# The first stage of a two-layer hybrid step: its own buffer for each scale and shift piece, and the first query and key products taken feature pair by feature pair

## The chip, the cores and the metric

The kernel runs on one core of a Trainium2 chip. The metric is the device time of one execution in microseconds (us); the time before is the median of three executions. The engines have the profile's names: PE multiplies matrices, with its weight loads shown apart as PEld; DVE, ACT and POOL work element by element; SP only issues loads and stores. Each of these runs its own instructions in a fixed order and waits for others through semaphores.

## The reference, cut to what matters

The step computes two layers over 512 latent tokens and 128 context tokens, 640 in all, of 1024 features. Layer 0 is attention, layer 1 a gated linear recurrence, and each is followed by a gated feed-forward block. What the change touches is the beginning of layer 0:

```
m  = silu(cond) @ w_mod + b_mod            # one row of conditions for latent, one for context tokens
shift, scale = first two parts of m        # 1024 each
xm = rms_norm(x, g) * (1 + scale) + shift
q, k, v = split(xm @ w_qkv)
```

`x` has 640 rows of 1024 features. `rms_norm` divides each token by the root of its mean square. Then queries, keys and values are made, 16 heads of 64, and attention follows.

## The kernel before, in words

Features lie on the 128 partitions, so that `x` is 8 tiles (k = 0 to 7) of 128 features by 640 tokens. A product of full precision is made of three products of numbers that are split into a high and a low part: high by high, high by low and low by high. This holds for all projections: the weights (`raw`) are split into `whi` and `wlo`, the tokens into `hi` and `lo` (all four token-wide arrays carry the tag `big` in the profile). A tile of 128 output features takes 8 k x 3 = 24 products for each half of the tokens (320 columns, the constant `CH`), 48 in all; `unit` loads and splits its weights, `some` (lines 214 to 223) makes the products. There are three slots each for `raw`, `whi` and `wlo`.

The first stage is `start` (lines 296 to 370). Its work:

- The features come in eight loads. ACT squares each, DVE adds the squares up (`ssq`). `stat` turns the sum into the root: PE sums over the partitions (`moment`, line 396), DVE scales, POOL takes the power, DVE spreads the result on a diagonal (`dg`), and PE multiplies it by ones so that every partition holds every token's factor (`spread`, line 413). The root is made in two pieces, latent and context, and copied to `ssq` by ACT.
- The scale and shift columns come from 16 pieces of `w_mod` of 512 KB each (`wm0`): four feature pairs (`NB` is 2) by shift or scale (j) by half of the sum (h). A piece is multiplied with the conditions in four small products (line 342), shift and scale in a bank each. The two halves go to `row` through DVE and ACT (lines 353 and 354), four products with `sel` turn the rows into columns (line 357), and small DVE operations give A and B, one column per feature and token kind. The 16 pieces share ten buffers.
- `scaled` gives each feature tile its scale and shift, one step behind the coefficients. Even tiles go through `modulate` on DVE and ACT (lines 418 to 420). Odd tiles are first multiplied by the root on POOL (line 350), then scaled on ACT (line 325) and split (`split`, lines 1076 and 1077).

Then the attention phase opens. `qk(0)` makes the first query tile Q and key tile K, `vq(0)` the first values (lines 236 to 238), and from there `attend(p)` (scores, softmax, output) goes on with `qk(p + 1)` and, at every other step, `vq` made beside it. Queries sit in one buffer with the tag `r`, keys in one with the tag `K` in the attention pool.

Which instruction stands where on each engine is set by the framework's scheduler: it takes program order as priority and orders by a simulated time. In `start` of the kernel before nothing is fixed by hand; `issue_after` is used elsewhere for single instructions.

## Time and profile before

| | |
|---|---|
| median of three executions | 1537.41 us (1535.1 to 1538.31) |
| span of the profiled execution | 1532.6 us |
| PE, DVE, ACT, POOL busy | 1483.2, 1062.8, 695.8, 256.1 us |
| first product of a scale or shift piece; first value product | at 12.8 us; at 57.6 us |

The page gives the span of the profiled execution, from its first to its last instruction; its time outside the span is not listed, and the median is 4.8 us above the span. PE is busy in 97% of the span, and a busy PE is not always PE at its peak, since the granted clock can be lower. In rows in order of time the first number is the start, the second the duration, and the bracket tells how long the engine idled before it and for what. Times of small products include their way through the array, so that the distance between two starts tells more than the duration. A product of plain float32 numbers (lines 342, 357, 396 and 413) shows as two records.

### The profile page before, as it was taken

The page shows a single profiled execution, that of the slowest core. Times are in us where ns is not written, and L with a number is a line of the kernel's source. Part 1 is how long each engine was busy: PE and PEld are TensorE (multiplying, and loading weights), DVE is VectorE, ACT ScalarE, POOL GpSimd, SP SyncE. Part 2 cuts the span into 40 slices and gives each one's busy share as a digit, 9 for nine tenths or more (in the row PEclk, how much of TensorE's full clock was granted, in tenths as well). Part 3 has the DMA queues.
Part 4 walks back from the last instruction along what each step waited for, and adds up shares of the span by engine and source line. Part 5 has one row for each costly group of instructions (what it writes and reads, how often), then busy time and mean ns, then how long its engine had stood idle before and what let it go on. Part 6 is the DMA issues. An engine that isn't in the chain of part 4 may idle for free.

```text
span 1532.6 us, 25990 instructions
## 1 busy us (share of the span) xinstructions
PE 1483.2 (97%) x10309; PEld 1438.5 (94%) x10309; DVE 1062.8 (69%) x2000; ACT 695.8 (45%) x1266; POOL 256.1 (17%) x270
## 2 busy tenths in 40 slices
PE   5999999989999999999999999999899999999997
PEld 4899999879999999999999988799899999999996
DVE  5668888969899888434443869885965656566556
ACT  5566767755333113312331478863534342424242
POOL 2101122100111110000000113230412323222210
PEclk8999999999999999999999999999999999999999
DMA  9545656445566664222223443334332231323221
GB/s 375 155 115 166 185 158 179 147 141 184 177 194 191 192 201 140 73 83 71 76 61 99 153 127 107 107 104 162 113 119 70 83 110 56 99 67 97 70 56 69
DMA packets 73098, 196.65 MB, mean 128 GB/s; under 512 B 8048, under 2 KB 25616, under 8 KB 72848
## 3 DMA queue, kind: packets, MB, share of 16 engines
q1 hardware_dynamic: 58832, 144.48, 30.0%
q0 software_dynamic: 13856, 50.35, 10.8%
q8 instruction: 81, 1.33, 0.4%
q14 instruction: 41, 0.34, 0.1%
q10 hardware_dynamic: 288, 0.16, 0.0%
HBM read 179.48 MB, written 8.92 MB: 123 GB/s over the span
## 4 chain that ended last, share of the span: by engine, by line
PE 85%; DVE 7%; ACT 4%; DMA 2%; issue 2%; SPq 0%; POOL 0%; POOLq 0%; DVEq 0%; ACTq 0%
PE mm L222 14%; PE mm L223 14%; PE mm L221 14%; PE mx L221 5%; PE mx L223 5%; PE mx L222 5%; PE mx L850 3%; PE mx L849 3%; PE mx L851 3%; PE op L687 2%; PE gp L1035 2%; PE tp L611 2%; PE mc L849 1%; PE mc L850 1%; PE mc L851 1%
## 5 line engine op out<-in xcount | busy, mean ns | idle before, releaser
L222 PE MATMUL mm<-big,whi 128*128 128x320 f32 (+3 forms) x1270 | 397.9, 314 | 3.0 <-DVE big L1077 2.1
L221 PE MATMUL mm<-big,whi 128*128 128x320 f32 (+3 forms) x1270 | 394.5, 313 | 3.7 <-ACT big L1076 2.3
L223 PE MATMUL mm<-big,wlo 128*128 128x320 f32 (+3 forms) x1270 | 396.8, 313 | 1.0 <-DVE wlo L182 1.0
L222 PEld LDWEIGHTS mm<-big,whi 128*128 128x128 f32 x1270 | 241.9, 190 | 6.6 <-DVE big L1077 4.4
L221 PEld LDWEIGHTS mm<-big,whi 128*128 128x128 f32 x1270 | 240.3, 190 | 7.5 <-ACT big L1076 2.8
L223 PEld LDWEIGHTS mm<-big,wlo 128*128 128x128 f32 x1270 | 241.5, 190 | 2.5 <-DVE wlo L182 1.4
L250 DVE SCALAR_TENSOR_TENSOR mprod<-mraw,csb 128x1024 f32<-128x1024 f32 x160 | 195.4, 1221 | 11.2 <-DMA mraw<-in_wm 10.7
L443 DVE SCALAR_TENSOR_TENSOR x<-mm,G,x 128x128 f32<-128x128 f32 (+3 forms) x205 | 83.5, 436 | 86.6 <-PE mm L223 86.6
L182 DVE TENSOR_TENSOR wlo<-raw,whi 128x1024 fp32r<-128x1024 f32 (+1 forms) x90 | 110.1, 1224 | 37.4 <-ACT whi L180 22.1
L180 ACT CAST whi<-raw 128x1024 fp32r<-128x1024 f32 (+1 forms) x74 | 76.8, 1037 | 110.1 <-PE mm L222 71.7
L221 PE MATMUL mm<-big,whx 128*128 128x320 f32 (+3 forms) x363 | 113.7, 313 | 0.0
L223 PE MATMUL mm<-big,wlx 128*128 128x320 f32 (+3 forms) x363 | 113.3, 312 | 0.0
L222 PE MATMUL mm<-big,whx 128*128 128x320 f32 (+3 forms) x363 | 113.1, 312 | 0.0
L246 POOL DMA_DIRECT2D mraw<-in_wm x80 | 43.3, 542 | 381.1 <-DVE mprod L250 264.9
L221 PE MATMUL mx<-big,whi 128*128 128x320 f32 (+3 forms) x298 | 93.5, 314 | 0.4 <-ACT big L1076 0.4
L223 PE MATMUL mx<-big,wlo 128*128 128x320 f32 (+3 forms) x298 | 93.0, 312 | 0.0
L222 PE MATMUL mx<-big,whi 128*128 128x320 f32 (+3 forms) x298 | 92.9, 312 | 0.0
L180 ACT CAST whx<-raw 128x1024 fp32r<-128x1024 f32 (+1 forms) x40 | 41.0, 1027 | 93.4 <-PE mm L222 54.2
L221 PE MATMUL mx<-big,whx 128*128 128x320 f32 (+3 forms) x245 | 75.6, 309 | 0.0
L223 PE MATMUL mx<-big,wlx 128*128 128x320 f32 (+3 forms) x245 | 75.5, 308 | 0.0
L1076 ACT CAST whi<-raw 128x1024 fp32r<-128x1024 f32 (+1 forms) x41 | 41.3, 1008 | 74.8 <-PE mm L222 45.0
L222 PE MATMUL mx<-big,whx 128*128 128x320 f32 (+3 forms) x245 | 75.2, 307 | 0.0
(301 smaller groups left out, 3620.8 us busy)
## 6 DMA issues: line engine op xcount, KB each, us to landing
raw<-in_gu SPq DMA_DIRECT2D x88, 512.0 KB, 3.6
mraw<-in_wm POOLq DMA_DIRECT2D x80, 512.0 KB, 4.0
raw<-in_dn SPq DMA_DIRECT2D x24, 512.0 KB, 3.7
raw<-in_wqk SPq DMA_DIRECT2D x16, 512.0 KB, 4.4
raw<-in_wi SPq DMA_DIRECT2D x16, 512.0 KB, 3.6
whi<-in_wi POOLq DMA_DIRECT2D x16, 512.0 KB, 4.0
raw<-in_dn SPq DMA_DIRECT2D x16, 448.0 KB, 3.4
sw<-in_wm SPq DMA_DIRECT2D x10, 512.0 KB, 10.5
```

What stands on the lines that cost most here:

```text
L180: nc.scalar.copy(hi, raw)
L182: nc.vector.tensor_tensor(lo, raw, hi.bitcast(F32), ALU.subtract)
L221: nc.tensor.matmul(ps, hi[:, k], xhi[:, k, s], start=(k == 0), stop=False)
L222: nc.tensor.matmul(ps, hi[:, k], xlo[:, k, s], start=False, stop=False)
L223: nc.tensor.matmul(ps, lo[:, k], xhi[:, k, s], start=False, stop=(k == last))
L246: nc.gpsimd.dma_start(w, self.i["wm"][l * 6 + j - 2, f])
L250: nc.vector.scalar_tensor_tensor(prod, w, 1.0, self.csb[:, s], ALU.mult, ALU.mult, accum_out=out[:, s, f:f + 1])
L443: self.nc.vector.scalar_tensor_tensor(xs, ps[:, a - t0:b - t0], G[:, s, f:f + 1], xs, ALU.mult, ALU.add)
L849: nc.tensor.matmul(ps, hi[:, k], xh[:, k], start=start and k == 0, stop=False, skip_group_check=not start)
L850: nc.tensor.matmul(ps, hi[:, k], xl[:, k], start=False, stop=False, skip_group_check=not start)
L851: nc.tensor.matmul(ps, lo[:, k], xh[:, k], start=False, stop=(k == KH - 1), skip_group_check=not start)
L1076: self.nc.scalar.copy(hi, v)
```

## The change

`start` is rewritten, with these parts:

- Each of the 16 pieces has its own buffer, and all loads are issued ahead: features, the four pieces of the first pair, the weights of the first query tile, first key tile and second query tile, and the other twelve pieces.
- Shift and scale of a pair go into the two halves of one bank, and the coefficients of a pair are made by three operations for both features. The root is made for all five token blocks at once, and the first pair is scaled from the bank that holds it.
- The order on PE, DVE and ACT is written out by hand: `pe`, `dve` and `act` make each instruction follow the one before it in that list on its engine.
- The first two query tiles and the first key tile are multiplied in six banks at once (three tiles by two halves of the tokens), pair by pair: for each pair first all high by high, then high by low, then low by high in two parts. After each of these four parts come the products of one piece of the next pair. Then the next pair's coefficients are made, it is scaled on DVE, cast on ACT, and its products follow.
- `qk` is cut into `queries`, `keys_tile` and the rest, so that `qk(0)` finds Q and K made, and `qk(1)` its query. The tag `r` gets two buffers, K moves to the main pool, and the memory for dynamic load descriptors is set to 4096.

The core of the diff:

```diff
@@ start
+        for k0 in range(0, KT, NB):
+            for j in range(2):
+                for h in range(2):
+                    w = self.t([P, 4, n], F32, f"sw{k0}{j}{h}", 1, sp)
+                    nc.sync.dma_start(w, self.i["wm0"][j, k0 // NB, h])
+                    pieces[k0, j, h] = w
+            if k0 == 0:
+                for f in (0, KT, 1):
+                    raw, whi_, wlo_ = [self.t([P, KT, P], dt, v, 3) for dt, v in ((F32, "raw"), (F32R, "whi"), (F32R, "wlo"))]
+                    nc.sync.dma_start(raw, self.i["wqk"][f])
+                    us.append((whi_, wlo_, raw))
...
+        def pe(step):
+            last["PE"] = order(step, (last.get("PE"),))
...
+        def vectors(k0, pm, j, h):
+            w = pieces[k0, j, h]
+            for k4 in range(4):
+                pe(lambda: nc.tensor.matmul(pm[32 * k4:32 * k4 + 32, j * n:j * n + n], csp[:, 4 * h + k4], w[:, k4], start=(h == 0), stop=(h == 1)))
+
+        def coefficients(k0, pm):
+            row = idle[:, k0 * n:k0 * n + 2 * n]
+            dve(lambda: nc.vector.tensor_copy(row[:, 0:n], pm[:, 0:n]))
+            act(lambda: nc.scalar.copy(row[:, n:2 * n], pm[:, n:2 * n]))
+            pt = self.ps("at")
+            for q in range(2 * NB):
+                pe(lambda: nc.tensor.matmul(pt[:, 2 * q:2 * q + 2], row[:, q * P:q * P + P], sel, start=True, stop=True))
...
+            dve(lambda: nc.vector.tensor_tensor(B, v[:, 0], per(self.col("bsh")), ALU.add))
+            dve(lambda: nc.vector.tensor_tensor(A, v[:, 1], per(b1), ALU.add))
+            dve(lambda: nc.vector.tensor_tensor(A, A, per(self.col("ng00")), ALU.mult))
+            return A, B
...
+        def normed(k, r):
+            dve(lambda: nc.vector.tensor_tensor(self.x[:, k], self.x[:, k], r, ALU.mult))
+
         def scaled(k, A, B):
             for s, a, b in _pieces(0, NTOK):
                 v = self.x[:, k, a:b]
+                dve(lambda: nc.vector.tensor_scalar(v, v, A[:, k % NB, s:s + 1], B[:, k % NB, s:s + 1], ALU.mult, ALU.add))
+            act(lambda: nc.scalar.copy(hi[:, k, 0:NTOK], self.x[:, k, 0:NTOK]))
+
+        def low(k):
+            dve(lambda: nc.vector.tensor_tensor(lo[:, k, 0:NTOK], self.x[:, k, 0:NTOK], hi[:, k, 0:NTOK].bitcast(F32), ALU.subtract))
+
+        def products(k, kind, js=range(6)):
+            for j in js:
+                w, m = us[j // 2][kind == "lh"], (lo if kind == "hl" else hi)
+                s = slice(*CH[j % 2])
+                first, end = kind == "hh" and k == 0, kind == "lh" and k == KT - 1
+                pe(lambda: nc.tensor.matmul(pss[j], w[:, k], m[:, k, s], start=first, stop=end))
+
+        pm = self.ps("ss")
+        vectors(0, pm, 0, 0)
+        bl, dg = root()
+        for j, h in ((0, 1), (1, 0), (1, 1)):
+            vectors(0, pm, j, h)
+        rr = spread(bl, dg)
+        A, B = coefficients(0, pm)
+        whi(0)
+        for k in range(NB):
+            for s, a, b in _pieces(0, NTOK):
+                v = self.x[:, k, a:b]
+                dve(lambda: nc.vector.scalar_tensor_tensor(v, v, A[:, k, s:s + 1], rr[s][:, 0:b - a], ALU.mult, ALU.mult))
+                act(lambda: nc.scalar.activation(hi[:, k, a:b], v, AF.Identity, bias=B[:, k, s:s + 1]))
+        whi(1)
+        r = copied(rr)
+        whi(2)
...
+        for j in range(3):
+            wlo(j)
+        pss = [(self.ps("kk") if j % 2 else self.pg(False))[:, 0:HT] for j in range(6)]
+        for k0 in range(0, KT, NB):
+            more = k0 + NB < KT
+            pm = self.ps("ss") if more else None
+            for step in range(4):
+                if step == 0:
+                    for k in range(k0, k0 + NB):
+                        products(k, "hh")
+                elif step == 1:
+                    for k in range(k0, k0 + NB):
+                        products(k, "hl")
                 else:
+                    for k in range(k0, k0 + NB):
+                        products(k, "lh", range(4) if step == 2 else range(4, 6))
+                if more:
+                    vectors(k0 + NB, pm, step // 2, step % 2)
+            if more:
+                for k in range(k0 + NB, k0 + 2 * NB):
+                    normed(k, r)
+                A, B = coefficients(k0 + NB, pm)
+                for k in range(k0 + NB, k0 + 2 * NB):
+                    scaled(k, A, B)
+                for k in range(k0 + NB, k0 + 2 * NB):
+                    low(k)
+        made = [self.queries(), self.keys_tile(), self.queries()]
+        for j in range(6):
+            t0, t1 = CH[j % 2]
+            made[j // 2][1](t0, slice(t0, t1), pss[j])
+        return [m[0] for m in made]
@@ run
-        with self.phase("start", at=2, rr=1, sc=1, sh=1) as sp:
+        with self.phase("start", at=1, ss=1, kk=3) as sp:
...
-            self.start(xhi, xlo, sp, wbig)
+            Q, K, Q1 = self.start(xhi, xlo, sp, wbig)
...
-            QK = self.qk(0, xhi, xlo, ap)
+            QK = self.qk(0, xhi, xlo, ap, Q, K)
...
-                    QK = self.qk(p + 1, xhi, xlo, ap)
+                    QK = self.qk(p + 1, xhi, xlo, ap, None if p else Q1)
@@ kernel
-    nc = _bacc.Bacc("TRN2", target_bir_lowering=False, num_devices=1)
+    nc = _bacc.Bacc("TRN2", target_bir_lowering=False, num_devices=1, dynamic_dma_scratch_size=4096)
```

`root`, `spread`, `copied`, `whi` and `wlo` do what `moment`, `spread`, line 347 and `unit` did, in the written order.

128 lines of the change are left out of this document (69 added, 59 removed).

## The prediction

> **What bounds the kernel now.** I read the page's first parts, then the stretches of ten microseconds, then the groups and the order of time of the first 60 us. In the page PE is busy nearly throughout:
>
> ```profile
> span 1532.6 us, 25990 instructions
> PE 1483.2 (97%) x10309; PEld 1438.5 (94%) x10309; DVE 1062.8 (69%) x2000; ACT 695.8 (45%) x1266; POOL 256.1 (17%) x270
> ```
>
> The span is 1532.6 us. The median of the three runs, 1537.4 us, is 4.8 us more; I take these 4.8 us as what lies around the span, and they stay. The stretches (length, then busy time of PE, PEld, DVE, ACT and POOL with their instructions, granted clock, DMA share, GB/s) show where PE becomes the bound:
>
> ```profile
> 30.00:40.00 10.00, 8.97 (x49) 6.82 (x48) 6.90 (x12) 6.19 (x9) 0.91 (x1) 0.66 1.02 410
> 40.00:50.00 10.00, 8.19 (x72) 6.12 (x70) 6.94 (x18) 5.83 (x11) 3.65 (x7) 1.00 0.38 117
> 50.00:60.00 10.00, 9.71 (x59) 9.72 (x60) 4.80 (x8) 4.89 (x10) 2.58 (x4) 0.83 0.65 197
> 60.00:70.00 10.00, 10.00 (x87) 10.00 (x86) 7.85 (x28) 5.18 (x9) 0.00 (x0) 1.00 0.57 156
> ```
>
> From 60 us on a stretch has 10.00 of 10.00 us of PE. So what the first stage is worth is the moment by which PE has put a given amount of projection work behind it; later work follows at PE's pace. In the groups of the first 60 us (busy us, then mean ns) the products of the first query and key tiles are counted:
>
> ```profile
> L222 PE MATMUL mm<-big,whi 128*128 128x320 f32 x32 | 12.0, 379 | 0.6 <-DVE big L420 0.6
> L223 PE MATMUL mm<-big,wlo 128*128 128x320 f32 x32 | 11.5, 370 | 1.0 <-DVE wlo L182 1.0
> L221 PE MATMUL mm<-big,whi 128*128 128x320 f32 x32 | 10.6, 387 | 0.8 <-ACT big L419 0.8
> ```
>
> That is 96, two tiles of 2 x 24 and 2 x 24. In the order of time (start, duration) stand two neighbours at half pace, two at full pace, and the last of the 96 with the first value product:
>
> ```profile
> 50.80 0.47 PE L221 MATMUL mm<-big,whi 128*128 128x320 f32 x1
> 51.07 0.47 PE L222 MATMUL mm<-big,whi 128*128 128x320 f32 x1
> ...
> 55.45 0.31 PE L221 MATMUL mm<-big,whi 128*128 128x320 f32 x1
> 55.59 0.31 PE L222 MATMUL mm<-big,whi 128*128 128x320 f32 x1
> ...
> 57.49 0.31 PE L223 MATMUL mm<-big,wlo 128*128 128x320 f32 x1
> 57.64 0.28 PE L236 MATMUL mm<-whi,big 128*128 128x256 f32 x1
> ```
>
> The 96 are done at 57.6 us. At full pace one follows the other after 0.147 us (three in 0.44), at half pace after 0.265. The changed stage also does the second query tile, 48 more, which before come later at full pace: 48 x 0.147 = 7.0. **The mark to compare with is 57.6 + 7.0 = 64.6 us for 144 products.**
>
> **The change, part by part.** The pairs of features are p0 to p3 (8 features, two at a time).
>
> *Up to the first scale and shift.* The rows before:
>
> ```profile
> 13.84 2.29 PE L396 MATMUL at<-ones,ssq 128*128 128x1 f32 x10
> ...
> 17.05 0.69 DVE L405 TENSOR_TENSOR dg<-ident,rs 128x512 f32<-128x512 f32 x1 [0.72 <-POOL rs L403]
> ...
> 18.78 1.63 PE L413 MATMUL rr<-dg,ones 128*128 128x128 f32 x8
> ...
> 20.45 0.59 ACT L347 COPY ssq<-rr 128x512 f32<-128x512 f32 x1 [1.16 <-PE rr L413]
> ...
> 21.25 0.61 PE L357 MATMUL at<-sel,big 128*128 128x2 f32 x4
> ...
> 21.90 0.28 DVE L363 TENSOR_SCALAR a<-at,b,cols 128x2 f32<-128x2 f32 x1 [1.10 <-PE at L357]
> ...
> 22.53 0.74 DVE L418 SCALAR_TENSOR_TENSOR big<-big,a,ssq 128x512 f32<-128x512 f32 x1
> ...
> 23.31 0.72 ACT L419 ACTIVATE big<-big,b 128x512 fp32r<-128x512 f32 x1 [2.28 <-DVE big L418]
> ...
> 23.94 0.24 ACT L347 COPY ssq<-rr 128x128 f32<-128x128 f32 x1
> ...
> 26.18 0.40 ACT L419 ACTIVATE big<-big,b 128x128 fp32r<-128x128 f32 x1 [1.99 <-DVE big L418]
> ...
> 26.74 1.04 ACT L180 CAST whi<-raw 128x1024 fp32r<-128x1024 f32 x1
> ```
>
> The five blocks' moments are already 10 records ending at 16.1. The diagonal is made at once for 640 instead of 512 columns, 0.69 x 640/512 = 0.86, and starts some 0.4 later, with the fifth block's moment, so it ends about 18.4, while PE, by the row at 18.78, is with the vectors until then: covered. The spread has 10 records instead of 8, 2.0 us, to 20.8; the four row turns (8 records, 2 x 0.6) to 21.9; then three small DVE operations instead of four. The first scaled feature starts at about 22.5, as it does now: no gain, no loss. ACT then has a fixed chain: two casts of 512 columns (0.72 each) and two of 128 (0.40), the second weights (1.04), the two copies of the root (0.59 + 0.24), the third weights (1.04): 23.3 + 2.2 + 1.0 + 0.8 + 1.0 = 28.4. PE's fixed order asks for the third weights after four products, so p0 runs from **28.5 us**.
>
> *One pair on PE.* 3 kinds x 2 features x 6 banks = 36 products, 36 x 0.147 = 5.3 us. Between them stand four blocks of vector products for the next pair. Rows for these and for what follows them:
>
> ```profile
> 18.91 0.37 ACT L354 COPY big<-sc 128x256 f32<-128x256 f32 x1 [6.68 <-PE sc L342]
> ...
> 23.19 0.42 DVE L353 COPY big<-sh 128x256 f32<-128x256 f32 x1
> ...
> 37.98 0.30 PE L223 MATMUL mm<-big,wlo 128*128 128x320 f32 x1
> ...
> 38.21 0.64 PE L342 MATMUL sc<-sw,csp 128*32 128x256 f32 x8
> ...
> 38.78 0.71 PE L221 MATMUL mm<-big,whi 128*128 128x320 f32 x3
> ```
>
> and from the groups of the whole run and of the first 60 us:
>
> ```profile
> L608 DVE TENSOR_SCALAR S<-S,rc 128x512 f32<-128x512 f32 x32 | 16.4, 513 | 0.6
> ...
> L638 DVE TENSOR_SCALAR S<-S,sm 128x128 f32<-128x128 f32 x16 | 4.3, 311 | 0.2
> ```
>
> ```profile
> L1076 ACT CAST big<-big 128x640 fp32r<-128x640 f32 x4 | 2.9, 718 | 0.0
> ```
>
> The last product before such a block starts at 37.98 and the next at 38.78: less the product's own 0.147 a block costs 0.65; the vector block is nearly the same kind of work in a fixed order, I take 0.6, so 2.4 a pair and 7.7 us in all. p0 has 32 products left at 28.5: 4.7 + 2.4 = 7.1, to 35.6 at full pace. PE has mostly waited since 22, so it starts at half pace (clock rows below): + 1.7, **p0 ends at 37.3 us**.
>
> *Between two pairs.* The fourth vector block comes after the pair's last product, and in PE's order the row turns and the next pair's products follow it. Nothing else can fill PE: the value weights have no slot, all three hold the two queries and the key. So PE waits out a chain: copies out of the bank 0.1 + 0.42; 8 records of turns 0.06 + 1.13 (two groups of 0.61 and 0.52); three DVE operations 0.5 (nearest, the row at 21.90: 0.63 later its fourth neighbour has started the next kind); scaling one feature 0.51 + 0.31 by the rows of 128x512 and 128x128; its cast on ACT 0.72; four handovers of some 0.05. **That is 3.9 us, three times.** From below: if the turns of the shift half run during the scale half's copy and the scaling runs at half of these rows, 2.8; from above 4.5, if the cast meets other work on ACT. I take 3.9, as the rows themselves give it. The second feature is ready 0.8 after the first and hides behind six products (0.9); the low parts hide behind the second six.
>
> *The sum.* 37.3 + 3 x 3.9 + 2 x 7.7 (p1, p2) + 5.3 (p3 has no vectors) = 69.7 us for the 144 products at full pace: 5.1 later than the mark.
>
> *The clock.*
>
> ```profile
> 26.00:28.00 2.00, 1.11 (x8) 1.09 (x12) 1.18 (x3) 1.82 (x4) 2.00 (x2) 0.66 1.07 434
> 46.00:48.00 2.00, 2.00 (x13) 1.67 (x12) 1.86 (x5) 1.67 (x3) 1.67 (x2) 1.00 0.57 181
> 48.00:50.00 2.00, 0.86 (x5) 0.48 (x3) 1.64 (x2) 1.18 (x3) 1.98 (x6) 1.00 0.34 81
> 50.00:52.00 2.00, 1.72 (x7) 1.72 (x8) 1.03 (x3) 0.00 (x0) 1.94 (x3) 0.63 0.94 262
> 52.00:54.00 2.00, 2.00 (x10) 2.00 (x9) 0.29 (x2) 0.87 (x3) 0.00 (x0) 0.52 1.01 353
> ```
>
> The columns are those of the stretches above. (1 - 0.63) x 2 x 2 = 1.5 us of 50 to 52 and 1.9 us of 52 to 54 are at half clock, 3.4 us together from 50.5 on, which cost 1.7. In the 3.4 us ahead of that PE was busy 0.9 (to 48) + 0.86 + some 0.2 = 2.0, more than half, and the clock fell all the same. At 26 to 28 it fell as well. A chain of 3.9 us with 1.1 us of short turns in it leaves a stretch of 3.4 us only a third busy if it falls inside, and some 60% busy only if an edge falls in the middle. I take two of three holes as followed by such a stretch: **+ 3.4**. Bounds: none, and three of twice the length (10.2).
>
> The Trainium skill ("TensorE: Matmul & The Clock Gate", Part 1) says that the clock goes to half after at least one idle window of about 3.4 us. Read strictly, a hole with turns in it holds no idle window, and the 3.4 us would fall away. The trace is against the strict reading: 2.0 of the 3.4 us before 50.5 were busy.
>
> *Value weights.* Now they lie ready when the queries and keys end. After the change their slots come free with the last products: the first low slot 4 products (0.6 us) before the end, and the subtraction is
>
> ```profile
> 33.51 1.21 DVE L182 TENSOR_TENSOR wlo<-raw,whi 128x1024 fp32r<-128x1024 f32 x1
> ```
>
> so the second value product is about 0.7 late; with ACT's casts of 1.04 and the copies out of six banks in the same moment I take **+ 1.0**, bounds 0 and 3.
>
> *At no cost.* The loads: 2.6 MB of features, 16 pieces and three weights are, by their shapes, 12.6 MB, 31 us at the 410 GB/s of the row at 30 to 40; the last piece is there by about 34, and p2's steps, which ask for it, come after 50. So the buffer for each piece takes away a wait that is not the next bound. SP issues the value weights, the cached keys and bias tables behind them, all needed after p3; if they came late, each weight tile of 512 KB takes 1.3 us. The six multiplications by the root on DVE (on POOL before for half of the features) run under 7.7 us of products; without that cover each adds about a cast of the same shape, 0.7. POOL is left free beside DVE, which helps p0 at most by what its 128-column operations took longer. The second buffer of the query rows and the smaller descriptor memory touch a queue whose engine is 17% busy: nothing.
>
> Total: 5.1 + 3.4 + 1.0 = 9.5 us later at the mark, and as PE is the bound behind it, 9.5 at the end: 1537.4 + 9.5 = **1546.9 us**.
>
> **The rivals.** (1) *Clock stays full after the holes*: 5.1 + 1.0 = 6.1, 1543.5 us. For it: the turns keep PE at work within the hole, and the clock stayed at 1.00 through 40 to 50 with 8.19 us busy; against it: the stretch 46 to 54. (The Trainium skill's rule, read strictly, would give this time.) (2) *The holes cost more*: three low stretches of twice the length and three for the value weights, 5.1 + 10.2 + 3 = 18.3, 1555.7. For it: the mean clock of 0.66 from 30 to 40, which is 6.8 us at half; against it: PE has no other waits inside p1 to p3. (3) *Short chain*: 2.8 a hole and p0 at full pace throughout, 35.6 + 8.4 + 15.4 + 5.3 = 64.7, + 1.0 - 64.6 = 1.1, 1538.5: no difference. (4) *Faster: the chain between pairs is hidden*, because DVE and ACT do their part while PE still streams the pair's last products. With 0 a hole and p0 as forecast: 37.3 + 20.7 + 1.0 - 64.6 = - 5.6, 1531.8. It decides at 1.9 us a hole; below that the change gains. Against it: the fourth vector block, without which no scale is complete, stands last in PE's order, and copy, turns and cast have the lengths of the rows. (5) *The change does not do what it says* would be a PE that in the first 60 us is as full as now with the same 96 products; the fixed order leaves no room for it, and it has no chance of its own.
>
> **How the numbers follow.** Forecast 0.43; (1) 0.18; (2) 0.11; (3) 0.10; (4) 0.18. 0.2% is 3.1 us, about what the three runs' spread lets one tell. Slower: 0.43 + 0.18 + 0.11 = 0.72; within: 0.10; faster: 0.18. The likeliest's own range is 1544 to 1551. The range of 1534 to 1556 leaves out (4) and the far end of (2).
>
> **What would show it.** Right: in the changed kernel's order of time PE runs p0 from about 28.5, three holes of about 4 us each between the groups of 36 products, with only turns in them; granted clock near 0.5 behind some; the 144th product at 70 to 75 us, and the DMA share falling from 1 before 36 us while PE waits on ACT and DVE, not on a load. Wrong: holes under 2 us, or a first value product before 64, would make the change a gain; PE under 10.00 of 10.00 between 80 and 250 us would mean that the second query's 48 products were missed as filler and the loss is greater.

## The result, and the profile after

| | before | after |
|---|---|---|
| median of the first comparison | 1535.80 us (6 executions) | 1543.99 us (6) |
| range | 1530.13 to 1538.31 | 1539.55 to 1547.18 |
| ratio | | 1.0064, 95% interval 1.0048 to 1.0081 |
| span of the profiled execution | 1532.6 us | 1545.4 us |
| a second comparison | 1534.17 us (15) | 1542.53 us (6), ratio 1.0057 (1.0036 to 1.0079) |
| span of its profiled executions | 1528.5 us | 1540.8 us |

The changed kernel is slower by 0.6%, some 8 to 9 us by the medians. (The ratios on record are not the quotients of the medians, 1.0053 and 1.0054; both intervals hold these too.) All twelve executions of it together have a median of 1542.6 us.

The page of the changed kernel (the span, and the engines' busy time, share and instructions):

```profile
span 1545.4 us, 25951 instructions
PE 1490.3 (96%) x10309; PEld 1442.6 (93%) x10309; DVE 1069.8 (69%) x2006; ACT 690.8 (45%) x1256; POOL 246.0 (16%) x265
```

PE does the same 10309 products as before. The stretches of ten microseconds (length, then busy time of PE, PEld, DVE, ACT and POOL with their instructions, granted clock, DMA share, GB/s):

```profile
30.00:40.00 10.00, 9.45 (x65) 6.42 (x64) 2.03 (x4) 0.37 (x1) 0.00 (x0) 0.78 1.02 414
40.00:50.00 10.00, 7.88 (x44) 6.09 (x43) 4.94 (x11) 3.25 (x3) 0.00 (x0) 0.66 0.38 119
50.00:60.00 10.00, 7.34 (x56) 5.49 (x56) 5.22 (x12) 1.82 (x3) 0.00 (x0) 0.92 0.12 29
60.00:70.00 10.00, 8.13 (x64) 5.46 (x56) 1.78 (x6) 0.37 (x1) 0.76 (x1) 0.91 0.00 0
70.00:80.00 10.00, 7.03 (x36) 6.77 (x36) 7.72 (x10) 4.57 (x7) 6.90 (x10) 0.83 0.30 105
80.00:90.00 10.00, 9.30 (x78) 9.30 (x79) 8.11 (x17) 8.90 (x20) 0.00 (x0) 1.00 0.85 241
90.00:100.00 10.00, 10.00 (x76) 9.82 (x76) 8.74 (x34) 5.42 (x11) 0.00 (x0) 1.00 0.37 108
```

PE is below 10.00 up to 90 us and full behind that: each stretch from 90 to 250 us has 10.00, so the sign that the prediction gave for a missing filler in attention isn't there. The DMA share has fallen by 40 to 50 and is nothing by 60: PE isn't waiting for a load. The list of PE's waits (engine, tile, line, then what it waited for: us in total, times, longest) says for what:

```profile
PE mm L421 <- ACT big L411: 7.7, 3, 3.5
```

The row with 7.7 us is three waits for ACT's cast of a pair's first feature. In order of time (start, duration; the bracket is the engine's idle time before it and what ended that) the second of the three holes:

```profile
52.77 0.64 PE L352 MATMUL ss<-sw,csp 128*32 128x256 f32 x8
...
53.48 0.42 DVE L356 COPY big<-ss 128x256 f32<-128x256 f32 x1 [7.94 <-PE ss L352]
53.94 0.37 ACT L357 COPY big<-ss 128x256 f32<-128x256 f32 x1 [8.94 <-DVE big L356]
...
53.96 1.05 PE L360 MATMUL at<-sel,big 128*128 128x2 f32 x8 [0.55 <-DVE big L356]
55.05 0.16 DVE L366 TENSOR_TENSOR b<-at,cols 128x4 f32<-128x4 f32 x1 [1.15 <-PE at L360]
...
55.52 1.51 DVE L410 TENSOR_SCALAR big<-big,a,b 128x512 f32<-128x512 f32 x4
56.35 1.44 ACT L411 CAST big<-big 128x640 fp32r<-128x640 f32 x2 [2.04 <-DVE big L410]
...
57.13 0.42 PE L421 MATMUL mm<-big,whi 128*128 128x320 f32 x1 [2.12 <-ACT big L411]
```

The last piece's products end at 53.41, and the next pair's first product starts at 57.13: 3.72 us, in which PE does 1.05 us of row turns. It is the chain that the prediction wrote down, link by link. One link wasn't foreseen: ACT's copy of the scale half stands behind DVE's copy of the shift half, out of the same bank (0.46 us from the one's start to the other's). It cost little here, since the first turns start at 53.96, beside ACT's copy. The first hole is as long (38.81 to 42.53), the third longer (67.08 to 72.14, 5.06 us, with an idle stretch of 3.47 us behind its turns). Then the clock behind the holes, in stretches of two microseconds with the same columns:

```profile
42.00:44.00 2.00, 1.47 (x5) 1.47 (x6) 1.92 (x5) 2.00 (x3) 0.00 (x0) 0.50 0.36 103
44.00:46.00 2.00, 2.00 (x8) 1.70 (x7) 1.54 (x3) 1.00 (x1) 0.00 (x0) 0.50 0.03 9
46.00:48.00 2.00, 2.00 (x12) 1.16 (x12) 0.00 (x0) 0.00 (x0) 0.00 (x0) 0.50 0.00 0
48.00:50.00 2.00, 2.00 (x18) 1.43 (x17) 0.00 (x0) 0.00 (x0) 0.00 (x0) 0.98 0.54 129
...
58.00:60.00 2.00, 2.00 (x12) 1.56 (x15) 2.00 (x3) 0.00 (x0) 0.00 (x0) 0.58 0.04 8
60.00:62.00 2.00, 2.00 (x14) 1.30 (x6) 0.14 (x1) 0.00 (x0) 0.00 (x0) 0.57 0.00 0
...
72.00:74.00 2.00, 1.86 (x7) 1.86 (x8) 2.00 (x2) 0.82 (x2) 1.98 (x5) 0.50 0.24 20
74.00:76.00 2.00, 2.00 (x11) 2.00 (x10) 1.90 (x2) 0.00 (x0) 2.00 (x2) 0.66 0.86 336
```

Behind every hole the granted clock goes to one half: for 3.4 us behind the second ((1 - 0.58) x 4 + (1 - 0.57) x 4), 3.4 behind the third, and 6 us of the three full rows behind the first, which with its edges make some 6.8, twice as long. The first of these stretches begins inside its hole (granted clock 0.83 in 38.81 to 42.53), so that some 1.3 us of it cost nothing. The end of the stage:

```profile
78.86 0.31 PE L421 MATMUL kk<-big,wlo 128*128 128x320 f32 x1
80.70 0.39 PE L236 MATMUL mm<-whi,big 128*128 128x256 f32 x1 [1.53 <-ACT r L644]
```

The 144th product starts at 78.86 and the first value product at 80.70. Against the prediction's mark (57.6 + 7.0 = 64.6 us) that is **16.1 us late**, while the whole program ends 12.8 us later in these two profiled executions and 8 to 9 us later by the medians.

### The profile page after: what moved, and what is told of

Same layout as the page of the kernel before. It is cut to its first block, busy times and chain, and to the rows that moved or that the text cites. A ratio compares the mean times of both kernels' runs of the same rounds, so it can differ in the third digit from the quotient of the medians.

```text
span 1545.4 us, 25951 instructions
## 1 busy us (share of the span) xinstructions
PE 1490.3 (96%) x10309; PEld 1442.6 (93%) x10309; DVE 1069.8 (69%) x2006; ACT 690.8 (45%) x1256; POOL 246.0 (16%) x265
## 5 line engine op out<-in xcount | busy, mean ns | idle before, releaser
L221 PE MATMUL mm<-big,whi 128*128 128x320 f32 (+3 forms) x1233 | 383.3, 312 | 2.4 <-ACT big L1190 2.0
L223 PE MATMUL mm<-big,wlo 128*128 128x320 f32 (+3 forms) x1233 | 384.7, 313 | 0.0
L222 PE MATMUL mm<-big,whi 128*128 128x320 f32 (+3 forms) x1233 | 383.8, 311 | 0.2 <-DVE big L1191 0.2
L221 PEld LDWEIGHTS mm<-big,whi 128*128 128x128 f32 x1233 | 232.7, 189 | 4.9 <-ACT big L1190 2.6
L222 PEld LDWEIGHTS mm<-big,whi 128*128 128x128 f32 x1233 | 233.4, 189 | 1.6 <-DVE big L1191 0.6
L223 PEld LDWEIGHTS mm<-big,wlo 128*128 128x128 f32 x1233 | 233.0, 189 | 0.8
L180 ACT CAST whi<-raw 128x1024 fp32r<-128x1024 f32 (+1 forms) x71 | 73.5, 1038 | 117.8 <-PE mm L222 71.8
L182 DVE TENSOR_TENSOR wlo<-raw,whi 128x1024 fp32r<-128x1024 f32 (+1 forms) x87 | 106.2, 1220 | 27.4 <-ACT whi L180 13.9
L221 PE MATMUL mm<-big,whx 128*128 128x320 f32 (+3 forms) x356 | 110.5, 310 | 0.0
L222 PE MATMUL mm<-big,whx 128*128 128x320 f32 (+3 forms) x356 | 110.1, 309 | 0.0
L221 PE MATMUL mx<-big,whi 128*128 128x320 f32 (+3 forms) x287 | 89.3, 311 | 0.0
L223 PE MATMUL mx<-big,wlo 128*128 128x320 f32 (+3 forms) x287 | 88.8, 310 | 0.0
L222 PE MATMUL mx<-big,whi 128*128 128x320 f32 (+3 forms) x287 | 88.6, 309 | 0.0
L221 PE MATMUL mx<-big,whx 128*128 128x320 f32 (+3 forms) x252 | 78.4, 311 | 0.0
L222 PE MATMUL mx<-big,whx 128*128 128x320 f32 (+3 forms) x252 | 78.1, 310 | 0.0
L1190 ACT CAST whi<-raw 128x1024 fp32r<-128x1024 f32 (+1 forms) x41 | 41.4, 1009 | 72.6 <-PE mm L222 44.9
```

The source lines that it names most:

```text
L180: nc.scalar.copy(hi, raw)
L182: nc.vector.tensor_tensor(lo, raw, hi.bitcast(F32), ALU.subtract)
L221: nc.tensor.matmul(ps, hi[:, k], xhi[:, k, s], start=(k == 0), stop=False)
L222: nc.tensor.matmul(ps, hi[:, k], xlo[:, k, s], start=False, stop=False)
L223: nc.tensor.matmul(ps, lo[:, k], xhi[:, k, s], start=False, stop=(k == last))
L1190: self.nc.scalar.copy(hi, v)
```

## The experiments

The first four ran beside one set of executions of the kernel before (26, median 1533.82 us, 1529.27 to 1538.35), the second four beside another (16, 1533.48 us), the last three beside a third (15, 1534.17 us). Each ratio is to its own set. The expectations also call DVE VectorE and POOL GpSimd.

**1. The vector blocks ahead of the pair's other products.** The two copies of `coefficients` become `rows` and stand right behind the blocks, the turns and the three small operations follow later. This is meant to take away the holes and leaves the six banks, the pairs and the fixed order.

```diff
-            for step in range(4):
-                if step == 0:
-                    for k in range(k0, k0 + NB):
-                        products(k, "hh")
...
-                if more:
-                    vectors(k0 + NB, pm, step // 2, step % 2)
+            for k in range(k0, k0 + NB):
+                products(k, "hh")
+            if more:
+                for step in range(4):
+                    vectors(k0 + NB, pm, step // 2, step % 2)
+                for k in range(k0 + NB, k0 + 2 * NB):
+                    normed(k, r)
+                rows(k0 + NB, pm)
+            products(k0, "hl")
+            if more:
+                A, B = coefficients(k0 + NB)
+            products(k0 + 1, "hl")
+            for js in (range(4), range(4, 6)):
+                for k in range(k0, k0 + NB):
+                    products(k, "lh", js)
```

> Changed kernel, but all four vector blocks of the next pair stand right behind the pair's high by high products, and the copies, turns, scaling and cast then run beside the remaining 24 products. Theory H (holes): the change is slower because PE waits three times for the chain copy, turns, coefficients, scaling, cast (3.7, 3.7 and 5.1 us in the trace of the changed kernel) and runs some 7 us worth slower at half clock behind it. H expects the three holes gone, the 144th product at 38.8 + 7.7 + 7.7 + 5.3 = 59.5 us instead of 79.0 and the first value product near 61 instead of 80.7, so 1526 to 1533 us, faster than the kernel before by 3 to 9. Theory F (filler): the loss arises in attention, where the second query's 48 products are missing as filler; it expects 1541 or more whatever the first stage does. Theory L (loads): the pieces or the value weights come late; it expects the holes to stay, with waits for loads in their place.

Measured: 1529.46 us (10 executions), ratio 0.9972 (0.9960 to 0.9984): a little faster than the kernel before, and 13 to 14.5 us faster than the changed one. Stretches of its profile:

```profile
30.00:40.00 10.00, 10.00 (x88) 7.74 (x84) 5.47 (x13) 2.67 (x4) 0.00 (x0) 0.86 1.02 412
40.00:50.00 10.00, 10.00 (x102) 8.25 (x94) 5.79 (x13) 3.00 (x5) 0.00 (x0) 1.00 0.48 143
50.00:60.00 10.00, 8.67 (x58) 7.88 (x57) 7.13 (x9) 2.55 (x4) 7.67 (x10) 1.00 0.29 105
```

From 30 to 50 us PE has 10.00 of 10.00: holes one and two are gone, and with them the half clock (1.00 in 40 to 50). The first value product comes at 63.00 us instead of 80.70. A piece of the third hole is left, two short waits. In order of time, DVE and POOL around it:

```profile
51.74 3.01 DVE L413 TENSOR_SCALAR big<-big,a,b 128x512 f32<-128x512 f32 x4
51.80 2.01 POOL L1257 MEMSET KZ<- 64x960 f32 x2 [34.43 <-DVE a L371]
...
54.69 3.78 DVE L417 TENSOR_TENSOR big<-big,big 128x640 fp32r<-128x640 f32 x2
55.92 3.62 POOL L777 TENSOR_TENSOR bt<-bt,mask 128x256 f32<-128x256 f32 x4
```

DVE's scaling takes 3.01 us where the same four instructions took 1.51 in the second hole, while POOL writes the zeros of the zero-padded keys and then of a bias table. The low parts take 3.78 us, and POOL adds masks beside them. (Run 7 takes this up.)

**2. Products in the holes.** Fourteen products whose result nothing reads go behind the row turns of each hole. They run where PE would be idle, so only the clock is changed.

```diff
+            if k0:
+                junk = self.ps("ss")[:, 0:HT]
+                for q in range(14):
+                    pe(lambda: nc.tensor.matmul(junk, us[0][0][:, 0], hi[:, 0, 0:HT], start=True, stop=True))
             B, A = [self.t([P, NB, 2], F32, v, 2, sp) for v in ("b0", "a0")]
```

> Changed kernel with 14 products that nobody reads put behind the turns in each of the three holes (14 x 0.147 = 2.1 us, about the wait that is left there). The holes stay as long as they are, only PE is at work in them. H in its form with the clock expects the granted clock near 1.00 from the first hole on, the 144th product at 79.0 less 4 to 7, and 1537 to 1541 us. If the half clock is not caused by the holes, or costs nothing, it stays at 1544 to 1547. F expects 1544 to 1547 as well.

Measured: 1542.47 us (10 executions), ratio 1.0054 (1.0037 to 1.0071). Stretches:

```profile
40.00:50.00 10.00, 10.00 (x80) 7.34 (x78) 4.54 (x8) 3.26 (x3) 0.00 (x0) 1.00 0.53 162
50.00:60.00 10.00, 9.45 (x73) 7.96 (x70) 5.37 (x12) 1.82 (x3) 0.00 (x0) 1.00 0.00 0
60.00:70.00 10.00, 7.54 (x58) 5.73 (x56) 6.47 (x10) 1.82 (x3) 5.51 (x8) 1.00 0.13 24
```

The clock is 1.00 throughout where the changed kernel has 0.66, 0.92 and 0.91, and the first value product comes at 75.63 instead of 80.70: so the stretches of half clock are the holes' doing. The holes stay as long as they were (3.72, 3.73 and 5.07 us). PE's rows in order of time, of p1 and p3:

```profile
41.60 0.41 PE L425 MATMUL mm<-big,whi 128*128 128x320 f32 x1
...
49.42 0.64 PE L352 MATMUL ss<-sw,csp 128*32 128x256 f32 x8
...
67.32 0.42 PE L425 MATMUL mm<-big,whi 128*128 128x320 f32 x1 [1.31 <-ACT big L415]
...
69.97 0.41 PE L425 MATMUL mm<-big,whi 128*128 128x320 f32 x1 [0.60 <-DVE big L418]
...
73.79 0.31 PE L425 MATMUL kk<-big,wlo 128*128 128x320 f32 x1
```

So at full clock p1 takes 8.46 us (41.60 to 50.06), p2 as much (53.79 to 62.25) and p3 6.6 (67.32 to some 73.9, with a wait of 0.60 for DVE's low parts in it), together 23.5 us. In the changed kernel they take 27.7 and 28.1 us in its two profiles: the half clock behind the holes costs 4.2 and 4.6 us at the mark. The 144th product ends at 73.9 instead of 79.0 us, within the expected 4 to 7 us; of these 5.1 us, 0.9 are gained ahead of the first hole. But the median is only 0.1 to 1.5 us below those of the changed kernel, 2.2 us by the two profiled spans: most of the gain at the mark doesn't arrive at the end. That part of the expectation (1537 to 1541) was missed.

**3. One query tile in the stage.** The second query's 48 products go back to where the kernel before has them; pairs, order and chain stay.

```diff
-        for f in (0, KT, 1):
+        for f in (0, KT):
...
-        def products(k, kind, js=range(6)):
+        def products(k, kind, js=range(4)):
...
-        return [m[0] for m in made]
+        return [m[0] for m in made] + [None]
```

> Changed kernel with only the first query and key tiles in the first stage, in four banks; the second query is made later, as in the kernel before. H expects the three holes to stay (3.7 to 5 us each), the 96th product at about 70 us against 57.6 in the kernel before, and the time within 3 us of the changed kernel: 1541 to 1547. F expects the filler back and so the time of the kernel before plus only the loss of the first stage; if F is the main cause, under 1539.

Measured: 1547.21 us (5 executions), ratio 1.0080 (1.0054 to 1.0107), just above the 1541 to 1547 that the holes were expected to give, and far from the time under 1539 that a missing filler was expected to give. The list of PE's waits has the same row as that of the changed kernel, 7.7 us in three waits for ACT's cast.

With one query the third slot of the weights is free, and twelve value products do come into the second hole (from 48.35 us, 1.5 us of work), but the pair behind it still waits until 52.95. The 96th product ends at about 73.6 us where the kernel before has 57.6, 16.0 us late: about the same loss as with three tiles, though in this profile each of the three stretches of half clock lasts 6.8 us (granted clock 0.69 in 36 to 47, 50 to 61 and 64 to 75). The holes and their loss are there without the third tile, and with it they don't go away.

**4. No fixed order.** The same program, with the list of what follows what on PE, DVE and ACT left out; the scheduler places the instructions.

```diff
-                    if ins is not None:
+                    if False:
                         st.enter_context(self.tc.issue_after(ins))
```

> Changed kernel, same instructions and same program order, without the order fixed by hand on PE, DVE and ACT: the scheduler places them. If the fixed order is what puts the chain behind the last products, the scheduler may take vector blocks earlier; H then expects shorter holes, a 144th product before 72 us and 1533 to 1541 us. If the order follows program order anyway, the holes stay and the time is 1543 to 1549.

Measured: 1530.33 us (10 executions), ratio 0.9975 (0.9962 to 0.9988), faster than either expectation (1533 to 1541, 1543 to 1549). PE's rows in order of time:

```profile
32.84 1.93 PE L352 MATMUL ss<-sw,csp 128*32 128x256 f32 x32
...
55.05 0.63 PE L421 MATMUL mm<-big,whi 128*128 128x320 f32 x1 [3.47 <-ACT big L411]
...
64.24 0.39 PE L236 MATMUL mm<-whi,big 128*128 128x256 f32 x1 [1.53 <-ACT r L644]
```

The row at 32.84 is all four vector blocks of p2 in one go, 32 records, ahead of p1's first product at 35.02; those of p1 ran from 21.4 us on, before and among the first products of p0. The scheduler has done by itself, for two of three pairs, what run 1 wrote out. The first two holes are gone, the third is there (3.47 us behind its turns; the last 14 of the 32 records of p3's blocks come at 48 to 50 us, among and behind p2's last products), and the value products start at 64.24. So the loss lies in the order that was written by hand; that it is the places of the vector blocks in it is shown by run 1.

**5. The kernel before, with a buffer for each piece.** The other part of the change by itself.

```diff
-        big = self.t([P, 5120], F32, "wb", 1, sp)
-        free = [big[:, j * D:j * D + D] for j in range(5)]
-        free = [self.t([P, D], F32, f"sw{j}", 1, sp) for j in range(5)] + free
+        free = [self.t([P, D], F32, f"sw{j}", 1, sp) for j in range(16)]
```

(The memory for dynamic descriptors is 4096 here too, as in the changed kernel; the space is needed.)

> The kernel before, with one part of the change alone: each of the 16 scale and shift pieces has a buffer of its own, and the order of the stage stays. My theory (the buffers take away a wait that is not the bound): the pieces arrive earlier, but the features of the later pairs wait for the products of the earlier ones or for vector work, so the time stays within 3 us of the kernel before and the first value product starts at 57 to 59 us. Rival (the waiting for a piece's buffer held the old stage back): the first value product comes at 52 to 55 us and the time falls by 3 to 5 us; then the loss of the changed kernel would be partly hidden by a gain from the buffers.

Measured: 1529.04 us (6 executions), ratio 0.9966 (0.9943 to 0.9989). PE's rows:

```profile
55.63 0.28 PE L236 MATMUL mm<-whi,big 128*128 128x256 f32 x1
```

The first value product comes at 55.63 us; in the kernel before at 57.64 and, in its second profile (run 9), at 56.15. In the first of these two profiles the clock is at half for 3.4 us from 50.5 on, in the second it isn't, nor here. So 0.5 to 2.0 us are gained at the mark, 0.5 where the clock is alike, where my theory had 57 to 59 us and the rival 52 to 55, and 4.4 us by the medians, where the theory had at most 3 and the rival 3 to 5. Neither holds whole. The interval excludes 1, but run 9 shows how far such an interval is to be trusted; a gain from these buffers is likely, its size open. Beside run 1 it says more: with the second query's 7.0 us the mark here is 62.6 us, where run 1 has its first value product at 63.0 and, repeated, at 63.9, and the medians are 1529.04 against 1529.46 and 1528.44. So no run shows that making the products pair by pair gains anything beyond what the buffers give by themselves.

**6. The small parts by themselves**: the kernel before with two buffers for the query rows, the key rows in the main pool, and 4096 for descriptors.

```diff
-        Q = self.t([P, NTOK], F32, "r", 1)
+        Q = self.t([P, NTOK], F32, "r", 2)
...
-        K = self.t([P, 960], F32, "K", 1, ap)
+        K = self.t([P, 960], F32, "K", 1)
...
-    nc = _bacc.Bacc("TRN2", target_bir_lowering=False, num_devices=1)
+    nc = _bacc.Bacc("TRN2", target_bir_lowering=False, num_devices=1, dynamic_dma_scratch_size=4096)
```

> The kernel before, with the other small parts alone: two buffers for the query rows, the key rows outside the attention stage's memory, and the smaller memory for descriptors. My theory: none of them is on the path, the time stays within 3 us of the kernel before. Rival (they change the order of the later stages and so where short gaps fall and the clock is lowered): a difference of 3 us or more, with the first value product where it was, 57 to 59 us, and another number of stretches of lower clock after 800 us.

Measured: 1532.88 us (10 executions), ratio 0.9995 (0.9975 to 1.0014), first value product at 57.60. No effect that these executions show, as expected.

**7. As run 1, with POOL's zeros later.** The zeros are made by a product that reads the first queries, so that they can't come before these.

```diff
-                nc.gpsimd.memset(self.kz[HD - a * HD:P - a * HD, a].bitcast(F32), 0.0)
+                z = slice(HD - a * HD, P - a * HD)
+                nc.gpsimd.tensor_scalar(self.kz[z, a], Q1[z, 0:1].broadcast_to([HD, 960]), 0.0, None, ALU.mult)
```

> As the kernel with the vector blocks ahead, but GpSimd writes the zeros of the zero-padded keys only once the first queries are there (by a product with zero that reads them), so that neither these nor the bias tables' zeros and masks run beside VectorE's scaling of the last pair. Theory (VectorE at half speed beside GpSimd is what is left of the third hole): the scaling of the last pair takes 1.5 us instead of 3.0, the low parts 1.6 instead of 3.8, the waits of 0.7 and 0.6 us go, the 144th product ends at about 60 us instead of 61.3, and the time is 1 to 2 us less than that of the kernel with the vector blocks ahead, about 1528 us. Rival 1 (the scaling is slow for a reason of its own, such as the memory it shares with the copies): it still takes 3 us, time the same. Rival 2 (the zeros are needed soon after): the first attention products wait, time 1530 to 1533 us.

Measured: 1525.87 us (4 executions), ratio 0.9941 (0.9921 to 0.9962), and run 1 once more in the same group 1528.44. DVE and POOL in order of time:

```profile
50.32 2.39 POOL L777 TENSOR_TENSOR bt<-bt,mask 128x256 f32<-128x256 f32 x4
...
51.28 0.88 DVE L371 TENSOR_TENSOR a<-a,cols 128x4 f32<-128x4 f32 x1
52.20 1.78 DVE L413 TENSOR_SCALAR big<-big,a,b 128x512 f32<-128x512 f32 x4
...
54.05 1.56 DVE L417 TENSOR_TENSOR big<-big,big 128x640 fp32r<-128x640 f32 x2
...
61.90 5.79 POOL L1258 TENSOR_SCALAR KZ<-r 64x960 fp32r<-64x960 f32 x2 [9.19 <-issue]
```

The scaling takes 1.78 instead of 3.01, the low parts 1.56 instead of 3.78, and the masks, which now run mostly alone, 2.39 instead of 3.62: DVE and POOL had held each other up in both directions. The stall isn't quite gone: the third small operation, beside the masks, takes 0.88 instead of 0.16, and of run 1's two short waits (0.7 and 0.6 us) one of 0.3 us is left. The first value product comes at 61.23 instead of 63.0 and 63.9. The median is 2.6 us lower, a little more than expected, and the lowest of the study, 0.6% below the kernel before; but the four executions (1525.64 to 1529.54) and the six of run 1's repetition (1525.31 to 1531.13) overlap, as do the two intervals, so that the gain is shown at the mark and only likely at the end.

**8. Run 1 once more.** The same kernel, no edit.

> The kernel with the vector blocks ahead once more, beside the others of this group: 1527 to 1531 us if its gain of 0.3% over the kernel before is its own, and 1533 or more if the first measurement was of a chip or an hour that favoured it. Its profile tells whether the recurrent layer again runs at full clock throughout (238 us from the layer's first instruction of that kind to the last layer's, where the kernel before has 246) or whether that differs from one execution to the next.

Measured: 1528.44 us (6 executions), ratio 0.9959 (0.9941 to 0.9978). The gain is there again; run 9 shows how much of it chance can make. From gate to snap (the first of the recurrent layer's gates to the first of the last layer's `snap` copies) it needs 240.3 us, in the first profile 238.2, so that stretch differs between executions of one kernel.

**9. The kernel before once more.** No edit.

> The kernel before once more, for a second profiled execution. In the first one the first attention outputs' last product starts at 330.6 us, the recurrent layer's first gate at 882.5 and the last layer's first snap at 1128.2: 245.7 from gate to snap, where the changed kernel's profile shows 241.0. Theory A (that stretch varies from one execution to the next, by short waits and the clock behind them, whatever the first stage): now 238 to 244 us, and the time of this execution is nearer to 1530. Theory B (the kernel before always needs about 246 there, because the order of its later instructions differs): 245 to 247 again.

Measured: 1532.02 us (10 executions), ratio to the kernel before, which is itself, 0.9983 (0.9969 to 0.9997). Two things follow. An interval that just excludes 1 isn't yet a difference: the same kernel gave one. And from gate to snap this execution needs 241.9 us (882.3 to 1124.2), where the first had 245.7: theory A. The 245.7 belonged to one execution. So did something nearer to the prediction: the pause of PE at 48 to 50 us is here too (0.87 us busy, 0.86 in the first profile), but the granted clock stays at 1.00 from 46 to 56 us, where the first profile has 0.63 and 0.52.

**10. The changed kernel once more.** No edit.

> The changed kernel once more, for a second profiled execution. The first stage should be the same to a few tenths: three holes of 3.7, 3.7 and 5.1 us, half clock behind each, the first value product at about 80.7 us. From the gate to the snap theory A gives anything from 238 to 246 us, theory B about 241. The ratio to the kernel before should be 1.005 to 1.008.

Measured: 1542.53 us (6 executions), ratio 1.0057 (1.0036 to 1.0079). The first products behind the holes and the first value product of this second profile:

```profile
40.57 0.42 PE L421 MATMUL mm<-big,whi 128*128 128x320 f32 x1 [2.12 <-ACT big L411]
...
69.24 0.63 PE L421 MATMUL mm<-big,whi 128*128 128x320 f32 x1 [3.47 <-ACT big L411]
...
78.85 0.39 PE L236 MATMUL mm<-whi,big 128*128 128x256 f32 x1 [1.36 <-ACT r L644]
```

The holes are the same, 3.72, 3.7 and 5.1 us. The expected 80.7 was missed by 1.9 us: the first pair ends that much earlier, with a granted clock of 0.79 from 20 to 36 us where the first profile has 0.68. Half clock now lasts 3.4 us behind the first and the second hole and 6.8 at the third. From gate to snap it is 240.2 us, which both theories allow.

**11. The changed kernel with only the zeros later**, the edit of run 7.

> The changed kernel with only GpSimd's zeros (and the bias tables behind them) moved behind the first queries. Theory (the third hole is longer because VectorE shares something with GpSimd there): the third hole falls from 5.1 to 3.7 us, the first value product comes at about 79.3 instead of 80.7, the time falls by about 1.4 us, to 1541 to 1544. If GpSimd's work is nothing to VectorE, the hole stays at 5.1.

Measured: 1547.51 us (4 executions), ratio 1.0084 (1.0066 to 1.0102). A miss. DVE and POOL in order of time:

```profile
67.48 2.38 POOL L773 TENSOR_TENSOR bt<-bt,mask 128x256 f32<-128x256 f32 x4
...
68.49 1.40 DVE L368 TENSOR_TENSOR a<-a,cols 128x4 f32<-128x4 f32 x1
69.92 1.52 DVE L410 TENSOR_SCALAR big<-big,a,b 128x512 f32<-128x512 f32 x4
...
71.51 1.56 DVE L414 TENSOR_TENSOR big<-big,big 128x640 fp32r<-128x640 f32 x2
```

DVE's scaling is back at 1.52 us and the low parts at 1.56, so POOL's work was what slowed them. But the masks, which had stood behind the zeros on POOL, now come at 67.48 and fall on the coefficients: the third small operation takes 1.40 us instead of 0.16 and ends with the last mask (69.89 and 69.86). The stall has moved by one link of the same chain, and the hole is 4.9 us long instead of 5.06. Why the time is 5 us above that of run 10 isn't settled: the first value product is 1.3 us later than in run 10, with the clock low for longer behind the first hole as in the first profile of the changed kernel, and another 2.4 us are lost before the last products of the attention outputs (347.9 against 344.2 us).

The "SBUF — State Buffer" page of the Trainium skill ("Who interferes with whom") says that VectorE's scaling by constants can use a port that it shares with GpSimd, that two inputs from SBUF (the on-chip memory that holds the tiles) contend with a GpSimd instruction that reads SBUF, and that the one that comes second is blocked for the whole instruction. Runs 1, 7 and 11 agree: 3.01 against 1.51 beside the writing of zeros, 3.78 against 1.56 beside the masks, and 1.40 against 0.16 for an operation of four columns.

## Why the prediction was right, and where it was not

The time (1546.9 forecast, 1543.99 measured), the direction and the mechanism were right. The terms weren't all, and errors have cancelled. By its time alone the result is nearer to rival (1), 1543.5, with the clock full behind the holes, and it lies at the lowest edge of the 1544 to 1551 given for the forecast itself; it is the trace, with half clock behind every hole, that decides for the forecast. That the sum came so near is in part luck. At the mark, from the trace of the changed kernel, with the pace at full clock from run 2:

| step | forecast | first profile | second profile |
|---|---|---|---|
| p0 ends, with its vector blocks | 37.3 us | 38.8 | 36.9 |
| three holes | 11.7 us | 12.5 | 12.5 |
| p1 to p3 at full clock (run 2) | 20.7 us | 23.5 | 23.5 |
| what half clock adds to them | 3.4 us | 4.2 | 4.6 |
| until the first value product | 1.0 us | 1.7 | 1.4 |
| first value product | 74.1 us | 80.7 | 78.9 |

(Half clock is what p1, p2 and p3 took between the holes, 10.9 + 9.95 + 6.9 = 27.7 us in the first profile and 9.94 + 9.93 + 8.25 = 28.1 in the second, less the 23.5 of run 2. The sign of a 144th product at 70 to 75 us was missed too: it ends at 79.0 and 77.5.)

*Up to the first scale and shift, and p0.* Nothing gained and nothing lost, as forecast: the third weights' products start at 28.24 us (forecast 28.5), and p0 ends within 1.5 us of the forecast in both profiles, later in the one with the longer half clock in p0.

*The holes.* 3.72 us against 3.9 for the first two: the chain was read rightly from rows of the kernel before. The third was mis-sized, 5.06 us, since DVE's scaling there takes twice its time beside POOL's zeros. The prediction said of POOL only that it is left free beside DVE; it looked at the first pair, not at what comes to stand beside the last one, when the attention phase's preparations begin. Run 1 confirms the holes as the cause by their removal, run 4 the order as what makes them, run 3 that the third tile is nothing to it.

*The pairs on PE.* "I take 0.6" for a vector block was too little, and this is the largest error of size between the holes: 23.5 us for p1 to p3 at full clock where 20.7 were summed. In run 2 a block stretches the row of products by 0.76 us (43.34 to 44.39 from the product before it to the second one behind it, less two of 0.147), since the first product behind it is slow as well, and p1 and p2 take 8.46 us instead of 7.7. In p3 the step "the low parts hide behind the second six" failed: DVE's low parts, slow beside POOL's masks, let PE wait 0.60 us in run 2, and p3 takes 6.6 instead of 5.3.

*The clock.* The mechanism was right, the size somewhat small. "I take two of three holes as followed by such a stretch" failed: all three were, in both profiles, and one of the three lasted 6.8 us instead of 3.4 in each (the first hole's in the first profile, the third's in the second), so that the sum was 13.6 us of half clock where 6.8 were forecast. They cost only 4.2 and 4.6 us, because a long one lay partly inside its hole and the one in p3 partly covers the wait for the low parts. The row that the forecast leaned on, the clock falling after a pause at 48 to 50 us, is not the rule either: in run 9 the same pause is followed by full clock. The rival with full clock falls; run 2 shows what it took to get it, products in the holes. The Trainium skill's rule ("TensorE: Matmul & The Clock Gate", Part 1), read strictly, asks for an idle window of about 3.4 us. Here holes of 3.72 us with 1.05 us of turns in them were enough, four times of four in the two profiles; only the third hole has a stretch of 3.47 us without any product. Its own addition that the window runs freely and isn't reset when the kernel starts agrees with the same hole being followed by 6.8 us in one execution and 3.4 in the other.

*Value weights.* 1.7 and 1.4 us instead of 1.0, but not for the weights: the bracket at 80.70 names ACT's copy out of a bank (L644). The copies stand behind the casts of the value weights on ACT, and PE waits for a free bank.

*At no cost: the buffer for each piece, "a wait that is not the next bound".* Doubtful after run 5: in the kernel before these buffers bring 0.5 to 2.0 us at the mark and some 4 at the end. That such a gain is covered by the chain in the changed kernel is argued, not shown. *The second buffer of the query rows and the descriptors' memory:* nothing, as forecast (run 6).

*"9.5 later at the mark, and 9.5 at the end."* This step failed twice. The mark came 16.1 us late, and what came late there did not all arrive at the end. The two pairs of profiles follow the loss through the program, by the first or last start of the same instruction before and after:

| | first pair of profiles | second pair |
|---|---|---|
| first value product, less 7.0 for the second query | 16.1 | 15.7 |
| last weight load for the attention outputs' products (`op<-PT,big`) | 17.2 | 14.1 |
| first gate of the feedforward part | 17.8 | 14.1 |
| first gate of the recurrent layer | 18.0 | 14.3 |
| first snap of the last layer | 13.3 | 12.6 |
| span | 12.8 | 12.3 |

The second query's 48 products are paid back about as reckoned (7.0): the raw difference is 23.1 us at the first value product and 17.2 by the end of attention in the first pair, 22.7 and 14.1 in the second. Of the 16 us, 3.3 and 3.4 are regained on the way, in the first pair between gate and snap: 245.7 us before and 241.0 after, of which PE idles 11.9 and 8.7. In the second pair PE idles 9.7 us there in both. From gate to snap thirteen profiles took between 238 and 246 us, the kernel before 245.7 and 241.9, that of run 1 238.2 and 240.3: it is a stretch in which executions differ, with no order by the first stage that I could find. That the medians differ by only 8 to 9 us where both pairs of profiles differ by 12 to 13 is in part a matter of which executions were profiled: the first one of the changed kernel (1547.18) is the slowest of its six, the second one of the kernel before (1530.46) the fastest of its ten. The rest stays open.

*The base.* I put 4.8 us around the span because the median of three executions stood that far above it. The executions with both numbers have 1.8 to 2.0 us there (1547.18 against 1545.4; 1530.46 against 1528.5), so the profiled execution itself was near 1534.5 (an estimate from its span), and the three executions happened to be slow ones: the larger sets have medians of 1533.5 to 1534.2. From that base the forecast's 9.5 us would have given 1544. So the forecast came near by a loss at the mark that was too small by 6.6 us (4.8 by the second profile), no account of the 3 us and more that are regained, and a base that was 3 us too high.

*The rivals.* The short chain falls: the holes were 3.7 and 5.1 us, not 2.8. Of the long low stretches of rival (2), one in three came in each profile of the changed kernel, and three in three in run 3's. Faster, "the chain between pairs is hidden": it did not happen here, but it is what happens as soon as the vector blocks move ahead. It gave 1531.8 us; run 1 measured 1529.46 and 1528.44. It was set against the changed kernel by the place of the fourth vector block, and that place decided.

## What to carry to other kernels

When work is cut into rounds on the bound engine, ask what stands between the last instruction of a round that feeds the side chain and the first that needs its result: here it was nothing, and a chain of 3.7 us on DVE and ACT came to stand in the open three times; moving four small blocks ahead of two thirds of the round's products turned a loss of 0.6% into a gain of 0.3 to 0.4%, though one part of the change, the buffers, measured as much alone (run 5). Price a hole on PE with the half clock behind it, which here was worth another third of the holes (4.2 and 4.6 us on 12.5). Size the round itself by a measured round, not by its products alone: here that was 2.8 us of the miss. And look at what the next phase's preparations on GpSimd will stand beside: moving them brought the mark 2 to 3 us ahead in run 7 and only shifted the stall by one link in run 11.

## What the runs showed of the chip that was not expected

- Two engines' copies out of the two halves of one bank ran one behind the other (DVE 53.48, ACT 53.94), in all four pairs: ACT's copy waits for DVE's. Whether they could have run together no run shows.
- GpSimd writing zeros beside DVE doubles DVE's scaling (1.51 to 3.01 us for four instructions); adding masks beside DVE's subtraction of two inputs costs both (1.56 to 3.78 us, and 2.38 to 3.62).
- Turns of two columns did not keep the clock up: 1.05 us of them in a hole of 3.72 us, and half clock behind it four times of four. Products of 320 columns for 2.30 us in the same holes did (1.00 in all three). How much work is enough no run shows: a pause with 0.86 and 0.87 us busy in 2 us was followed by half clock in one profile of the kernel before and by full clock in the other.
- The same kernel measured twice gave a ratio of 0.9983 with an interval that excludes 1.
